# A masked row sum with a loop of as many rounds as the lengths need: addresses worked out on one partition, rests behind the first blocks, TensorE's program on a 256 boundary

## The chip, the cores and the metric

One core of one Trainium2 chip. The metric is the device time of the kernel in microseconds (us), the median of several runs; each timed run stands beside runs of the kernel before on the same chip.

## The reference

```python
B, S, D = 8, 8192, 512
x: (B, S, D) float32, lengths: (B,) in 16..S-1, w: (D, D) float32
masked = x * (pos < lengths)
cs = cumsum(masked, axis=1)
out = cs[b, lengths[b] // 2, :] @ w          # (8, 512)
```

So row b of the result is the sum of the first n[b] = min(lengths[b]//2 + 1, lengths[b]) rows of x[b], times w. For this draw n is 570, 2690, 256, 2057, 905, 3772, 3859, 571. The kernel reads only these rows: whole blocks of 512 rows (1 MB), and rests of under 512 rows.

## The kernel before

TensorE sums a block with matmuls whose stationary operand is a column of weights (which of the 8 rows the block belongs to). The first block of rows 0 and 1 is loaded blind, before the lengths are known. One block of row 7 is loaded into a tile `last` at the end. All other blocks are "places": 7 buffers, used in rounds of 7. With these lengths there are 25 places (the two blind ones and 23 more), so four rounds hold them; the longest lengths need nine.

```python
BLIND, NS = 2, 7
ROUNDS = -(-(B * S // 2 // BLK - 1) // NS)          # 9
...
# SyncE: loads
sp.wait_ge(s_dve, DVE_ADDR)
sp.load(facts, meta[:])                              # how many places, ...
with sp.Fori(0, ROUNDS):
    sp.load(at, addr[:, off:off + NS])               # seven addresses to registers
    nested(sp, left, NS, load_item)                  # load_item waits for s_free[k], starts a DMA
    ...
    sp.wait_ge(s_dve, DVE_ALL)
... then the two halves of `last`
# VectorE, before the loops: n_f (lengths to counts, one partition); TensorE broadcasts them to
# 128 partitions (n_ps); then on 128 partitions
step(dve.tensor_copy, out=cnt[:], in_=n_ps[:, :B])
step(dve.tensor_scalar, out=blocks[:], in0=cnt[:], ...)
... has, usual, begin, step_a, since, part_a, sum_a, addr[0:7], meta x3      # = DVE_ADDR
... bit masks for the rests, since for all places, wtab (weights of all places)   # = DVE_MASK
# GpSimd: waits for n_f, then memset of the second rest buffer (128 x 2048)
# TensorE
pe.wait_ge(s_dve, DVE_MASK)
with pe.Fori(0, ROUNDS):
    with pe.If_cmp(rest_rounds, 1, "IS_GE"): ...     # the rests of two rows, 8 matmuls
    nested(pe, left, NS, add_item)   # add_item: 2 idle matmuls, wait s_full[k], 4 matmuls
    ...
tell()                               # a tiny matmul that signals VectorE: the sum is complete
... first half of last; fold of the copied sum; second half of last; product with w
```

`keep_busy` in front of each place is a pair of idle matmuls, meant to keep TensorE's clock up (in the nine rounds below, one more pair in each round took the tail from 4.20 us to 3.33). A float32 matmul appears in the trace as two passes: 8 records for the 4 of a place, 16 for the 8 of two rests.

## Time and profile before

| | before |
|---|---|
| time, median of the runs | 93.1 us (93.07 to 94.05) |
| span of the profiled run | 90.7 us |
| DMA | 345 GB/s mean over the span, 419 to 420 while it streams |
| TensorE busy | 53.3 us (59%) |
| last two DMAs of `last` landed | 78.73 and 79.96 us |
| output issued | 87.8 us |

How to read it: the share of busy time says little here. What counts is whether DMA streams without gaps to its end, and how long the chain is from the last landing to the output. The lines are in the prediction below.

### The profile page before, as it was taken

The page shows a single profiled execution, that of the slowest core. Times are in us where ns is not written, and L with a number is a line of the kernel's source. Part 1 is how long each engine was busy: PE and PEld are TensorE (multiplying, and loading weights), DVE is VectorE, ACT ScalarE, POOL GpSimd, SP SyncE. Part 2 cuts the span into 40 slices and gives each one's busy share as a digit, 9 for nine tenths or more (in the row PEclk, how much of TensorE's full clock was granted, in tenths as well). Part 3 has the DMA queues.
Part 4 walks back from the last instruction along what each step waited for, and adds up shares of the span by engine and source line. Part 5 has one row for each costly group of instructions (what it writes and reads, how often), then busy time and mean ns, then how long its engine had stood idle before and what let it go on. Part 6 is the DMA issues. An engine that isn't in the chain of part 4 may idle for free. (4 is left out here: it accounts for less than half of the span.)

```text
span 90.7 us, 1568 instructions
## 1 busy us (share of the span) xinstructions
PE 53.3 (59%) x387; PEld 11.6 (13%) x391; DVE 17.5 (19%) x86; ACT 3.7 (4%) x5; POOL 3.0 (3%) x11
## 2 busy tenths in 40 slices
PE   0730006999999994242668993354659966404840
PEld 0400001111112110000012110010112111003520
DVE  3787886010101110000000110000000000003220
ACT  3900000000000000000000000000000000000020
POOL 5700000000000000000000000000000000000000
PEclk9999999999999999999999999999999999997597
DMA  2899989999999999999999999999999999400000
GB/s 29 340 416 426 369 288 413 437 419 416 434 408 423 416 423 430 415 395 426 412 423 430 416 416 430 408 426 416 419 423 426 419 419 407 177 2 0 0 0 7
DMA packets 4837, 31.28 MB, mean 345 GB/s; under 512 B 674, under 2 KB 690, under 8 KB 1218
## 3 DMA queue, kind: packets, MB, share of 16 engines
q1 hardware_dynamic: 3906, 27.27, 73.0%
q10 hardware_dynamic: 928, 3.97, 11.3%
q8 instruction: 1, 0.02, 0.1%
q14 instruction: 2, 0.02, 0.0%
HBM read 31.23 MB, written 0.02 MB: 345 GB/s over the span
## 5 line engine op out<-in xcount | busy, mean ns | idle before, releaser
L430 PE MATMUL s_ps<-xt,cur 128*8 128x512 f32 x200 | 26.1, 593 | 16.5 <-PEq L131 16.4
L430 PE MATMUL s_ps<-rem,cur_rem 128*8 128x512 f32 x64 | 9.3, 707 | 9.1 <-PEq L131 9.1
L443 PE MATMUL idle_ps<-idle 128*128 128x512 bf16 x46 | 14.2, 384 | 0.6 <-issue 0.6
L404 DVE COPY cur<-wtab 128x8 f32 x18 | 3.1, 171 | 36.3 <-DVEq L131 36.3
L430 PEld LDWEIGHTS s_ps<-xt,cur 128*8 128x8 f32 x200 | 3.4, 87 | 27.8 <-issue 27.8
L443 PEld LDWEIGHTS idle_ps<-idle 128*128 128x128 bf16 x50 | 2.8, 97 | 22.3 <-issue 22.3
L289 DVE COPY s_sb<-s_ps 128x256 f32<-128x256 f32 x2 | 0.8, 425 | 21.7 <-PE idle_ps L447 21.7
L262 ACT COPY o_sb<-o_ps 8x128 f32<-8x128 f32 x2 | 0.5, 260 | 82.5 <-PE o_ps L504 82.5
L430 PEld LDWEIGHTS s_ps<-rem,cur_rem 128*8 128x8 f32 x64 | 1.8, 95 | 15.8 <-issue 15.7
L447 PE MATMUL idle_ps<-idle 128*1 128x1 bf16 x1 | 0.2, 163 | 4.2 <-issue 4.2
L451 PE MATMUL n_ps<-n_f,ones 1*128 1x8 f32 x2 | 0.6, 366 | 2.9 <-DVE n_f L289 2.9
L436 PE MATMUL t_ps<-last,e_last 128*8 128x128 f32 x32 | 2.3, 414 | 0.0
L397 DVE COPY cur_rem<-table 128x32 f32 x6 | 1.1, 182 | 5.8 <-DVEq L131 5.8
L452 PE MATMUL s_ps<-zero 1*128 1x512 f32 x2 | 2.0, 1126 | 0.0
L214 ACT ACTIVATE rem<-rem 128x2048 uint32<-128x2048 uint32 x1 | 1.9, 1910 | 0.0
L278 POOL MEMSET rem<- 128x2048 f32 x1 | 1.8, 1805 | 0.8 <-DVE n_f L289 0.8
L504 PE MATMUL o_ps<-wt,t_sb 128*8 128x128 f32 x32 | 1.2, 304 | 0.4 <-DVE t_sb L289 0.4
L214 ACT ACT_TABLE_LOAD x1 | 1.3, 1283 | 1.3 <-PEq L525 1.3
L436 PEld LDWEIGHTS t_ps<-last,e_last 128*8 128x8 f32 x32 | 1.3, 121 | 0.2
L289 DVE TENSOR_TENSOR wtab<-since 128x504 f32<-128x504 f32 x1 | 1.1, 1066 | 0.0
L289 DVE TENSOR_TENSOR part_a<-since,step_a 1x49 f32<-1x49 f32 (+1 forms) x2 | 1.1, 529 | 0.1
L504 PEld LDWEIGHTS o_ps<-wt,t_sb 128*8 128x8 f32 x32 | 0.9, 98 | 1.0 <-issue 0.9
(62 smaller groups left out, 14.3 us busy)
## 6 DMA issues: line engine op xcount, KB each, us to landing
xt<-in_x_dram SPq DMA_DIRECT2D x25, 1024.0 KB, 16.6
rem<-in_x_dram ACTq DMA_DIRECT2D x3, 512.0 KB, 7.5
wt<-in_w_dram ACTq DMA_DIRECT2D x1, 1024.0 KB, 4.9
last<-in_x_dram SPq DMA_DIRECT2D x2, 512.0 KB, 6.9
rem<-in_x_dram ACTq DMA_DIRECT2D x3, 256.0 KB, 7.0
rem<-in_x_dram ACTq DMA_DIRECT2D x3, 128.0 KB, 6.7
rem<-in_x_dram ACTq DMA_DIRECT2D x3, 32.0 KB, 5.5
rem<-in_x_dram ACTq DMA_DIRECT2D x1, 64.0 KB, 7.2
```

Source lines behind the costliest of these rows:

```text
L214: act.memzero(rem[:, 0]).then_inc(s_rfree[0], 1)
L262: copy = act.copy(out=o_sb[1][:, j * P:(j + 1) * P], in_=o_ps[64 + 32 * j:64 + 32 * j + B, :P])
L278: pool.memset(rem[:, 1], 0.0).then_inc(s_rfree[1], 1)
L289: do(*args, **kw).then_inc(s_dve, 1)
L397: dve.tensor_copy(out=cur_rem[:, q], in_=rests[:, ds(dve.snap(at, min_val=1, max_val=B // 2 - 1), 1), q].rearrange("p o w -> p (o w)"),).t ...
L404: dve.tensor_copy(out=cur[:, k], in_=wtab[:, ds(dve.snap(at, min_val=1, max_val=ROUNDS - 1), 1), k].rearrange("p o b -> p (o b)"),).then_i ...
L430: return pe.matmul(s_ps[32 * j:32 * j + B], lhsT=weights, rhs=rows, start=False, stop=False, skip_group_check=True, tile_position=(0, 32 * j))
L436: return pe.matmul(t_ps[32 * j:32 * j + B, :P], lhsT=weights, rhs=row[:, P * j:P * (j + 1)], start=False, stop=False, skip_group_check=Tru ...
L443: pe.matmul(idle_ps[:], lhsT=idle[:, :P], rhs=idle[:], start=True, stop=True)
L451: pe.matmul(n_ps[:, :B], lhsT=ones[:], rhs=n_f[:], start=True, stop=True).then_inc(s_pe, 1)
L452: pe.matmul(s_ps[:], lhsT=zero[:], rhs=zero[:, :1].to_broadcast((1, D)), start=True, stop=False, skip_group_check=True)
L504: mm = pe.matmul(o_ps[32 * j:32 * j + B, :P], lhsT=t_sb[:, kc, :B], rhs=wt[:, kc, j * P:(j + 1) * P], start=(kc == 0), stop=(kc == KC - 1) ...
```

## The change

Its intent: no empty rounds; first addresses sooner; the two blind blocks used first, so that their buffers come free early; and TensorE's program put on a 256 boundary, with the product in a block of its own and a branch hint. Cut to its core:

```diff
-        sp.wait_ge(s_dve, DVE_ADDR)
-        sp.load(facts, meta[:])
-        with sp.Fori(0, ROUNDS):
+        sp.wait_ge(s_dve, DVE_ADDR)
+        sp.load([left] + at[BLIND:], addr[:, BLIND - 1:NS])
+        nested(sp, left, NS, load, BLIND)
+        sp.wait_ge(s_dve, DVE_ALL)
+        sp.load(facts, meta[:])
+        with sp.Fori(1, facts[1]):                      # rounds needed, at least 4
 # GpSimd
-        pool.wait_ge(s_dve, DVE_N)
+        pool.wait_ge(s_dve, DVE_ADDR)
         pool.memset(rem[:, 1], 0.0)
 # VectorE
+        begins(n_i, blocks1, has1, usual1, begin1)      # on one partition, straight from n_i
+        ... step_a, since, part_a, sum_a, addr for five places    # = DVE_ADDR, step 21 (was 28)
+        step(dve.tensor_copy, out=n_f[:], in_=n_i[:])   # = DVE_N, step 23 (was 11)
+        ... bit masks; cnt; begins() on 128 partitions; weights of round 0 (no table wtab any more)
+        ... number of rounds = max(4, rounds with a place in them) into meta
 # TensorE
+        pe.addr_align(256, offset=0, max_nops=0)
+        hint = pe.mark_branch_hint_location()
-        with pe.Fori(0, ROUNDS):
+        with pe.Fori(0, rounds):
+            nested(pe, left, BLIND, add_item)
             ... rests of two rows
-            nested(pe, left, NS, add_item)
+            nested(pe, left, NS, add_item, BLIND)
-        ... product
+        pe.br("product")
+        with nc.body("product", ...): ... product; pe.br("product_end").branch_hint(hint)
```

VectorE's refills follow the same order (weights of two places, rests, weights of five).

More of the change, by code (lines that the diff above doesn't have):

```diff
@@ L6 @@
 from concourse._compat import with_exitstack
+from concourse.ordered_engine_set import OrderedEngineSet
 F32 = mybir.dt.float32
@@ L80 @@
     idle = sb("idle", [P, D], BF16)
-    cnt = sb("cnt", [P, B], I32)
-    blocks = sb("blocks", [P, B], I32)
     special = sb("special", [P, B])
-    has = sb("has", [P, B])
-    usual = sb("usual", [P, B])
     one8 = sb("one8", [P, B])
-    begin = sb("begin", [P, B + 1])
+    cnt, blocks, has, usual, begin = [sb(n, [P, B + (n == "begin")], I32 if n in ("cnt", "blocks") else F32)
+                                      for n in ("cnt", "blocks", "has", "usual", "begin")]
+    blocks1, has1, usual1, begin1 = [sb(n + "1", [1, B + (n == "begin")], I32 if n == "blocks" else F32)
+                                     for n in ("blocks", "has", "usual", "begin")]
     step_c = sb("step_c", [1, B - 1])
@@ L96 @@
     addr = sb("addr", [1, ITEMS], I32)
-    meta = sb("meta", [1, 3], I32)
-    wtab = sb("wtab", [P, ROUNDS, NS, B])
+    left_f = sb("left_f", [1, ROUNDS])
+    round_f = sb("round_f", [1, 1])
+    meta = sb("meta", [1, 4], I32)
     cur = sb("cur", [P, NS, B])
@@ L142, in less @@
         eng.reg_alu(n, n, 0, ALU.max)
-    DVE_SEL, DVE_N, DVE_ADDR, DVE_MASK, DVE_ALL = 2, 11, 28, 51, 56
+    DVE_SEL, DVE_ADDR, DVE_N, DVE_MASK, DVE_ALL = 2, 21, 23, 56, 64
     DVE_LAST = DVE_ALL + 6
@@ L168, in _, with load @@
         at = [sp.alloc_register(f"sp_at{k}") for k in range(NS)]
-        facts = [sp.alloc_register(f"sp_fact{k}") for k in range(3)]
-        sp.reg_mov(off, 0)
+        facts = [sp.alloc_register(f"sp_fact{k}") for k in range(4)]
+        sp.reg_mov(off, NS)
+        def load(k):
+            take(sp, s_free[k], 1)
+            sp.dma_start(
+                out=xt[:, k], in_=xf[ds(sp.snap(at[k]), BLK)].rearrange("(p g) d -> p g d", g=G)
+            ).then_inc(s_full[k], 16)
         sp.wait_ge(s_dve, DVE_ADDR)
+        sp.load([left] + at[BLIND:], addr[:, BLIND - 1:NS])
+        nested(sp, left, NS, load, BLIND)
+        sp.wait_ge(s_dve, DVE_ALL)
         sp.load(facts, meta[:])
-        sp.reg_mov(left, facts[0])
-        with sp.Fori(0, ROUNDS):
-            sp.load(at, addr[:, ds(sp.snap(off, min_val=0, max_val=ITEMS - NS), NS)])
-            def load(k):
-                take(sp, s_free[k], 1)
-                sp.dma_start(
-                    out=xt[:, k], in_=xf[ds(sp.snap(at[k]), BLK)].rearrange("(p g) d -> p g d", g=G)
-                ).then_inc(s_full[k], 16)
-            def load_item(k):
-                if k < BLIND:
-                    with sp.If_cmp(off, 1, "IS_GE"):
-                        load(k)
-                else:
-                    load(k)
-            nested(sp, left, NS, load_item)
+        with sp.Fori(1, sp.snap(facts[1], min_val=B // 2, max_val=ROUNDS)):
+            sp.load(at, addr[:, ds(sp.snap(off, min_val=NS, max_val=ITEMS - NS), NS)])
             less(sp, left, NS)
+            nested(sp, left, NS, load)
             sp.reg_alu(off, off, NS, ALU.add)
             sp.reg_alu(off, off, ITEMS - NS, ALU.min)
-            sp.wait_ge(s_dve, DVE_ALL)
-        with sp.If_cmp(facts[1], 1, "IS_GE"):
-            from_rows = xf[ds(sp.snap(facts[2]), BLK)].rearrange("(p g) d -> p g d", g=G)
+        with sp.If_cmp(facts[2], 1, "IS_GE"):
+            from_rows = xf[ds(sp.snap(facts[3]), BLK)].rearrange("(p g) d -> p g d", g=G)
             for h in range(2):
@@ L307, in _, with begins, sinces @@
         step(dve.tensor_scalar, out=n_i[:], in0=n_i[:], scalar1=1, scalar2=None, op0=ALU.add)
-        step(dve.tensor_tensor, out=n_f[:], in0=n_i[:], in1=lens1[:, ::2], op=ALU.min)
-        assert done == DVE_N, done
-        step(dve.memset, since[:, :1], 1.0)
-        step(dve.memset, since[:, B:], 0.0)
-        step(dve.memset, e_last[:], 0.0)
-        step(dve.memset, e_last[:, B - 1:], 1.0)
-        dve.wait_ge(s_pe, 1)
-        step(dve.tensor_copy, out=cnt[:], in_=n_ps[:, :B])
-        step(dve.tensor_scalar, out=blocks[:], in0=cnt[:], scalar1=9, scalar2=None,
-             op0=ALU.logical_shift_right)
-        step(dve.scalar_tensor_tensor, out=has[:], in0=blocks[:], scalar=1.0, in1=special[:],
-             op0=ALU.is_ge, op1=ALU.mult)
-        step(dve.tensor_tensor, out=usual[:], in0=blocks[:], in1=has[:], op=ALU.subtract)
-        step(dve.tensor_tensor_scan, out=begin[:, 1:], data0=one8[:], data1=usual[:], initial=float(BLIND),
-             op0=ALU.mult, op1=ALU.add)
-        step(dve.scalar_tensor_tensor, out=step_a[:], in0=usual[:1, :B - 1], scalar=float(-BLK), in1=step_c[:],
-             op0=ALU.mult, op1=ALU.add)
+        step(dve.tensor_tensor, out=n_i[:], in0=n_i[:], in1=lens1[:, ::2], op=ALU.min)
+        def begins(cnt, blocks, has, usual, begin):
+            parts = blocks.shape[0]
+            step(dve.tensor_scalar, out=blocks[:], in0=cnt[:], scalar1=9, scalar2=None,
+                 op0=ALU.logical_shift_right)
+            step(dve.scalar_tensor_tensor, out=has[:], in0=blocks[:], scalar=1.0, in1=special[:parts],
+                 op0=ALU.is_ge, op1=ALU.mult)
+            step(dve.tensor_tensor, out=usual[:], in0=blocks[:], in1=has[:], op=ALU.subtract)
+            step(dve.tensor_tensor_scan, out=begin[:, 1:], data0=one8[:parts], data1=usual[:],
+                 initial=float(BLIND), op0=ALU.mult, op1=ALU.add)
+        def sinces(begin, a, b):
+            parts = begin.shape[0]
+            step(dve.tensor_tensor, out=since[:parts, 1:B, a:b],
+                 in0=shape(item[:parts, a:b].unsqueeze(1), parts, B - 1, b - a),
+                 in1=shape(begin[:, 1:B].unsqueeze(2), parts, B - 1, b - a), op=ALU.is_ge)
         def addresses(a, b):
@@ L332, in addresses @@
             step(dve.tensor_tensor, out=addr[:, a:b], in0=item_a[:, a:b], in1=sum_a[:, a:b], op=ALU.add)
-        def sinces(parts, a, b):
-            step(dve.tensor_tensor, out=since[:parts, 1:B, a:b],
-                 in0=shape(item[:parts, a:b].unsqueeze(1), parts, B - 1, b - a),
-                 in1=shape(begin[:parts, 1:B].unsqueeze(2), parts, B - 1, b - a), op=ALU.is_ge)
+        begins(n_i, blocks1, has1, usual1, begin1)
+        step(dve.tensor_copy, out=addr[:, BLIND - 1:BLIND], in_=begin1[:, B:])
+        step(dve.scalar_tensor_tensor, out=step_a[:], in0=usual1[:, :B - 1], scalar=float(-BLK), in1=step_c[:],
+             op0=ALU.mult, op1=ALU.add)
         dve.wait_ge(s_pool, 1)
-        sinces(1, 0, NS)
-        addresses(0, NS)
-        step(dve.tensor_copy, out=meta[:, :1], in_=begin[:1, B:])
-        step(dve.tensor_copy, out=meta[:, 1:2], in_=has[:1, B - 1:])
-        step(dve.tensor_scalar, out=meta[:, 2:], in0=blocks[:1, B - 1:], scalar1=BLK,
-             scalar2=(B - 1) * S - BLK, op0=ALU.mult, op1=ALU.add)
+        sinces(begin1, BLIND, NS)
+        addresses(BLIND, NS)
         assert done == DVE_ADDR, done
+        step(dve.memset, since[:, :1], 1.0)
+        step(dve.tensor_copy, out=n_f[:], in_=n_i[:])
+        assert done == DVE_N, done
         step(dve.memset, bits[:], 256)
@@ L362, in _ @@
         step(dve.tensor_tensor, out=thr[:, 2:], in0=thr_i[:], in1=shape(m4[:], P, 2), op=ALU.mult)
+        step(dve.memset, since[:, B:], 0.0)
+        dve.wait_ge(s_pe, 1)
+        step(dve.tensor_copy, out=cnt[:], in_=n_ps[:, :B])
+        begins(cnt, blocks, has, usual, begin)
+        sinces(begin, 0, ITEMS)
+        step(dve.tensor_tensor, out=cur[:].rearrange("p k b -> p b k"), in0=since[:, :B, :NS],
+             in1=since[:, 1:, :NS], op=ALU.subtract)
+        step(dve.memset, cur[:, :BLIND], 0.0)
+        step(dve.tensor_copy, out=cur[:, :BLIND].rearrange("p k b -> p (k b)")[:, ::B + 1], in_=has[:, :BLIND])
         step(dve.memset, table[:], 0.0)
@@ L370, in _ @@
         step(dve.tensor_copy, out=cur_rem[:], in_=rests[:, 0])
-        sinces(P, 0, ITEMS)
-        step(dve.tensor_tensor, out=wtab[:].rearrange("p r k b -> p b (r k)"), in0=since[:, :B],
-             in1=since[:, 1:], op=ALU.subtract)
-        step(dve.memset, wtab[:, 0, 1, :1], 0.0)
-        for b in range(BLIND):
-            step(dve.tensor_copy, out=wtab[:, 0, b, b:b + 1], in_=has[:, b:b + 1])
-        step(dve.tensor_copy, out=cur[:], in_=wtab[:, 0])
-        step(dve.memset, t_ps[:, :P], 0.0)
+        step(dve.tensor_copy, out=meta[:, :1], in_=begin1[:, B:])
+        step(dve.tensor_scalar, out=left_f[:], in0=item[:1, :ROUNDS], scalar1=float(-NS), scalar2=begin1[:, B:],
+             op0=ALU.mult, op1=ALU.add)
+        step(dve.tensor_scalar, out=left_f[:], in0=left_f[:], scalar1=1.0, scalar2=None, op0=ALU.is_ge)
+        step(dve.tensor_reduce, out=round_f[:], in_=left_f[:], axis=mybir.AxisListType.X, op=ALU.add)
+        step(dve.tensor_scalar, out=meta[:, 1:2], in0=round_f[:], scalar1=float(B // 2), scalar2=None, op0=ALU.max)
+        step(dve.tensor_copy, out=meta[:, 2:3], in_=has1[:, B - 1:])
+        step(dve.tensor_scalar, out=meta[:, 3:], in0=blocks1[:, B - 1:], scalar1=BLK,
+             scalar2=(B - 1) * S - BLK, op0=ALU.mult, op1=ALU.add)
         assert done == DVE_MASK, done
         addresses(NS, ITEMS)
+        step(dve.memset, t_ps[:, :P], 0.0)
+        step(dve.memset, e_last[:], 0.0)
+        step(dve.memset, e_last[:, B - 1:], 1.0)
         step(dve.tensor_scalar, out=fold_i[:], in0=fold_i[:], scalar1=31, scalar2=None,
@@ L386, in _, with weights @@
         dve.wait_ge(s_dve, done)
-        left, at, rest_rounds = [dve.alloc_register(f"dve_{n}") for n in ("left", "at", "rests")]
-        dve.load([left], meta[:, :1])
-        dve.reg_mov(at, 1)
+        left, rounds, at, of, rest_rounds = [dve.alloc_register(f"dve_{n}") for n in ("left", "rounds", "at", "of", "rests")]
+        dve.load([left, rounds], meta[:, :2])
+        dve.reg_mov(at, NS)
+        dve.reg_mov(of, 1)
         dve.reg_mov(rest_rounds, B // 2 - 1)
-        with dve.Fori(1, ROUNDS):
+        with dve.Fori(1, dve.snap(rounds, min_val=B // 2, max_val=ROUNDS)):
             less(dve, left, NS)
+            def weights(k):
+                take(dve, s_done[k], 1)
+                here = ds(dve.snap(at, min_val=NS, max_val=ITEMS - NS) + k, 1)
+                dve.tensor_tensor(
+                    out=cur[:, k], in0=since[:, :B, here].rearrange("p b o -> p (b o)"),
+                    in1=since[:, 1:, here].rearrange("p b o -> p (b o)"), op=ALU.subtract,
+                ).then_inc(s_free[k], 1)
+            nested(dve, left, BLIND, weights)
             with dve.If_cmp(rest_rounds, 1, "IS_GE"):
@@ L398, in _ @@
                         out=cur_rem[:, q],
-                        in_=rests[:, ds(dve.snap(at, min_val=1, max_val=B // 2 - 1), 1), q].rearrange("p o w -> p (o w)"),
+                        in_=rests[:, ds(dve.snap(of, min_val=1, max_val=B // 2 - 1), 1), q].rearrange("p o w -> p (o w)"),
                     ).then_inc(s_rfree[q], 1)
-            def weights(k):
-                take(dve, s_done[k], 1)
-                dve.tensor_copy(
-                    out=cur[:, k],
-                    in_=wtab[:, ds(dve.snap(at, min_val=1, max_val=ROUNDS - 1), 1), k].rearrange("p o b -> p (o b)"),
-                ).then_inc(s_free[k], 1)
-            nested(dve, left, NS, weights)
+            nested(dve, left, NS, weights, BLIND)
             less(dve, rest_rounds, 1)
-            dve.reg_alu(at, at, 1, ALU.add)
-            dve.reg_alu(at, at, ROUNDS - 1, ALU.min)
+            dve.reg_alu(at, at, NS, ALU.add)
+            dve.reg_alu(at, at, ITEMS - NS, ALU.min)
+            dve.reg_alu(of, of, 1, ALU.add)
+            dve.reg_alu(of, of, B // 2 - 1, ALU.min)
         dve.wait_ge(s_pe, PE_ALL)
@@ L448, in tell, with add_item @@
                       stop=True).then_inc(s_pe, 1)
+        pe.addr_align(256, offset=0, max_nops=0)
+        hint = pe.mark_branch_hint_location()
+        pe.wait_ge(s_dve, DVE_SEL)
+        pe.matmul(s_ps[:], lhsT=zero[:], rhs=zero[:, :1].to_broadcast((1, D)), start=True,
+                  stop=False, skip_group_check=True)
         pe.wait_ge(s_dve, DVE_N)
         pe.matmul(n_ps[:, :B], lhsT=ones[:], rhs=n_f[:], start=True, stop=True).then_inc(s_pe, 1)
-        pe.matmul(s_ps[:], lhsT=zero[:], rhs=zero[:, :1].to_broadcast((1, D)), start=True,
-                  stop=False, skip_group_check=True)
         pe.wait_ge(s_pool, 2)
         pe.wait_ge(s_dve, DVE_MASK)
-        left, has_last = pe.alloc_register("pe_left"), pe.alloc_register("pe_has")
+        left, rounds, has_last = [pe.alloc_register(f"pe_{n}") for n in ("left", "rounds", "has")]
         rest_rounds = pe.alloc_register("pe_rests")
-        pe.load([left, has_last], meta[:, :2])
+        pe.load([left, rounds, has_last], meta[:, :3])
         pe.reg_mov(rest_rounds, B // 2)
-        with pe.Fori(0, ROUNDS):
+        with pe.Fori(0, pe.snap(rounds, min_val=B // 2, max_val=ROUNDS)):
+            def add_item(k):
+                keep_busy()
+                take(pe, s_full[k], 16)
+                for j in range(G):
+                    mm = add(j, cur[:, k], xt[:, k, j])
+                mm.then_inc(s_done[k], 1)
+            nested(pe, left, BLIND, add_item)
             with pe.If_cmp(rest_rounds, 1, "IS_GE"):
@@ L466, in _ @@
                     mm.then_inc(s_rdone[q], 1)
-            def add_item(k):
-                keep_busy()
-                take(pe, s_full[k], 16)
-                for j in range(G):
-                    mm = add(j, cur[:, k], xt[:, k, j])
-                mm.then_inc(s_done[k], 1)
-            nested(pe, left, NS, add_item)
+            nested(pe, left, NS, add_item, BLIND)
             less(pe, left, NS)
@@ L498, in _ @@
             tell()
-        pe.wait_ge(s_w, 16)
-        for kc in range(KC):
-            if kc % 2 == 0:
-                pe.wait_ge(s_dve, DVE_ALL + 3 + kc // 2)
-            for j in range(4):
-                mm = pe.matmul(o_ps[32 * j:32 * j + B, :P], lhsT=t_sb[:, kc, :B],
-                               rhs=wt[:, kc, j * P:(j + 1) * P],
-                               start=(kc == 0), stop=(kc == KC - 1), tile_position=(0, 32 * j))
-        mm.then_inc(s_pe, 1)
+        pe.br("product")
+        with nc.body("product", valid_engines=OrderedEngineSet([mybir.EngineType.PE])):
+            pe.wait_ge(s_w, 16)
+            for kc in range(KC):
+                if kc % 2 == 0:
+                    pe.wait_ge(s_dve, DVE_ALL + 3 + kc // 2)
+                for j in range(4):
+                    mm = pe.matmul(o_ps[32 * j:32 * j + B, :P], lhsT=t_sb[:, kc, :B],
+                                   rhs=wt[:, kc, j * P:(j + 1) * P],
+                                   start=(kc == 0), stop=(kc == KC - 1), tile_position=(0, 32 * j))
+            mm.then_inc(s_pe, 1)
+            pe.br("product_end").branch_hint(hint)
+        nc.switch_bb("product_end")
     block.__exit__(None, None, None)
```

## The prediction

> **What bounds the kernel now.** I read the busy slices first, then stretches of time, the chain of waits, the timeline of the first 13 us, and the branches of TensorE. The kernel streams rows of x from HBM in places of 512 rows (1 MB), seven to a round, and adds them up on TensorE.
>
> Slices and stretches (span, PE, PEld, DVE, ACT, POOL busy; clock; DMA share; GB/s):
>
> ```profile
> DMA  2899989999999999999999999999999999400000
> 9.07:11.30 2.23, 0.00 (x0) 0.00 (x0) 1.94 (x7) 0.00 (x0) 0.00 (x0) 1.00 1.02 375
> 11.30:13.60 2.30, 0.00 (x0) 0.00 (x0) 2.00 (x7) 0.00 (x0) 0.00 (x0) 1.00 0.80 284
> 18.10:66.00 47.90, 33.76 (x229) 5.67 (x232) 3.99 (x23) 0.00 (x0) 0.00 (x0) 1.00 1.01 419
> 78.20:82.80 4.60, 0.45 (x7) 0.00 (x0) 0.00 (x0) 0.00 (x0) 0.00 (x0) 1.00 0.03 11
> 82.80:87.80 5.00, 3.83 (x73) 2.68 (x73) 1.91 (x6) 0.52 (x2) 0.00 (x0) 0.66 0.00 0
> ```
>
> From 2.3 to 78.2 us the DMA engines are full at 419 GB/s, except for one dip at 9 to 13.6 us. Then 4.6 us pass in which neither DMA nor TensorE has much to do, and the last 5 us run at a mean clock of 0.66. So there are three places where time can be had: the dip, the hole and the slow tail.
>
> The chain of waits (start, length, what):
>
> ```profile
> 77.61 1.05 PE s_ps L430 x8
> 78.65 4.18 issue
> 82.83 0.16 PE idle_ps L447
> 82.99 2.45 PE t_ps L436 x40
> ...
> 85.87 1.29 PE o_ps L504 x32
> ```
>
> The hole is 4.18 us of "issue" on TensorE: no wait, only its sequencer. The loop runs nine rounds. The lengths of this draw give 25 places plus one block that goes to `last`, so four rounds hold them all and five are empty. The branches of the loop show the five (operation, count, duration in ns min/median/max, first and last start):
>
> ```profile
> L461 PEldq COMPARE_BRANCH  x9: 64/201/201, 14.2 to 82.0; - x9
> L460 PEldq COMPARE_BRANCH  x9: 69/201/223, 27.8 to 82.7; - x9
> ```
>
> In an empty round three branches are taken at 201 ns each, with the register operations and gaps some 0.92 us per round in the trace (back edges at 78.05, 79.01, 79.93, 80.84, 81.75 and 82.71). Five make 4.65 us, of which 0.5 lies under the last matmuls.
>
> The dip: timeline of the address chain, the competing memset and SyncE's loads:
>
> ```profile
> 2.90 1.80 POOL L278 MEMSET rem<- 128x2048 f32 x1 [0.82 <-DVE n_f L289]
> 3.59 0.17 DVE L289 CAST cnt<-n_ps 128x8 int32<-128x8 f32 x1
> 3.79 0.94 DVE L289 TENSOR_SCALAR blocks<-cnt 128x8 int32<-128x8 int32 x1
> 4.77 0.17 DVE L289 SCALAR_TENSOR_TENSOR has<-blocks,special 128x8 f32<-128x8 int32 x1
> ...
> 10.04 3.09 SPq L179 DMA_DIRECT2D xt<-in_x_dram  x5
> ...
> L175 SPq TENSOR_LOAD <-addr x9: 934/1467/1488, 8.2 to 70.5; - x9
> ...
> 72.13 0.87 SPq L200 DMA_DIRECT2D last<-in_x_dram  x2
> DMA to landing us min/median/max: 6.6/6.9/7.3
> ```
>
> The first computed place is issued at 10.04, its data flow from about 12.0, but the two blind blocks are through at 10.3. And `last` is issued only at 72.13, 10.2 us after the last place (61.61), because SyncE too walks five empty rounds with a register load in each. It lands at 78.73 and 79.96, still before TensorE wants it at 82.98.
>
> [...]`blocks` took 944 ns where others of 128x8 take 168, and ended at 4.74, when the memset (2.90 + 1.80) ended. [...]the clock records have 0.5 from 82.88 to 86.29, right after the hole. [...] The TensorE trace before shows no such stall (empty rounds are 0.92 us each, all alike), so its alignment and branch hint have nothing visible to remove[...].
>
> **The change part by part.**
>
> *Addresses from one partition.* The chain no longer passes through TensorE (broadcast, then copy `cnt`) and no longer runs beside the memset, which now waits for the addresses. From the end of `n_f` at 2.85: ten steps on one partition at about 0.19 us (their durations are 0.14 to 0.23 plus 0.035 gap) make DVE_ADDR near 4.9 instead of 7.04. SyncE then loads one set of six registers (0.9) instead of two sets (877 and 946 ns), and skips the two pairs of branches for blind places. First issue: 4.95 + 0.9 + 0.3 = 6.2 instead of 10.04; its data flow from about 8.1, before 10.3. So the dip closes: lost bytes are (419-375) x 2.23 + (419-284) x 2.30 = 409 KB, at 419 GB/s **0.98 us** earlier for everything the stream delivers.
>
> *What this gives back.* The 1.8 us memset now starts near 5.0 and should block the cast of `n_f` until about 6.8. VectorE then has 33 further steps to DVE_MASK. With their measured durations (twelve bit steps 2.14, since 0.65, cur 0.25 instead of wtab's 1.07, table to cur_rem 1.0, seven small meta steps 1.3 and the rest) I get 13.7, against 13.08 before. TensorE starts near 15.2 instead of 14.48. That is off the path: it starts with the blind blocks, so place 0 is free near 17.6, and SyncE, after DVE_ALL near 16.1 and two register loads, reissues at about 18.6, against 20.31 before. The queue then has bytes until about 23.
>
> *Rests behind the blind blocks.* Moves 3.6 us of cold matmuls from ahead of the first place; frees two places earlier and delays the next rest loads by some 3 us. They have slack: rests of round 1 landed by 26.94 and would be used after 30. Worth 0 by itself.
>
> *Rounds as needed.* Four rounds instead of nine. The tell follows the last matmul at once: -4.02 us of the hole. VectorE and SyncE lose their empty rounds too; `last` is issued near 62, but queued behind the same bytes, so it lands with the end of the stream: 79.96 - 0.98 = 79.0.
>
> *Tail, worked out.* Last place lands at 77.47 - 0.98 = 76.5; its matmuls end at 77.65; tell 77.8; s_sb copies (2 x 0.425) end at 78.7; first half of `last` in between; fold to 78.95; second half at 79.0. With no hole the clock stays full, so those 16 matmuls start within 0.45 us instead of 0.8 and end at 79.65, against 85.43 before: 5.78 us earlier. The product has 8 of its 32 matmuls at half clock now: about 0.15 less, perhaps 0.3 with its first weight load. The rest (copies, output, end) is as before, 5.25 - 0.2. Span: 79.65 + 5.05 = 84.7. The timed figure is 93.1 for a span of 90.7; adding the same 2.4 gives **87.1**, I put 87.0.
>
> In parts: dip 1.0, hole net of the new wait for `last` and of overlap about 3.8, full clock in the tail about 1.2: 6.0.
>
> **The rivals.** (a) *A fetch stall takes the place of the empty rounds.* With them gone the exit runs straight from a loop of some 215 instructions into new code. For it: [...]that the author adds alignment and a hint. Against it: the back edges at 28.3, 48.9 and 68.3 show no stall[...].[...] (b) *The stream's end doesn't move*, because the memset, the later TensorE start or later rests open another dip at 20 to 25 us. The margin (reissue 18.6, bytes until 23) speaks against it; then 88. (c) *The end of `last` is later*, since it now sits 10 us longer in the queue among rests: at most some tenths, 87.5. (d) *The nine rounds were hidden under the stream anyway*: the hole is after the stream's end at 78.2, and only 1.8 us of it lie before `last` lands at 79.96; then the 2.9 us from 79.96 to 82.83 are still gained, and the time could not be above 90.3.
>
> **Range and chances.** Centre 87.0. Everything as worked out, or a bit better in the end sequence, gives 86; rival (b)[...] 88 to 89.2. Range 85.9 to 89.3. Faster by over 2% needs under 91.2[...]: 0.97; within 2%: 0.02; slower: 0.01.
>
> **What would show it.** Right: DMA share full in the slices of 9 to 13.6 us; first place issued near 6.2; no long idle ahead of the tell; clock 1.0 until the product; `last` issued near 62 and TensorE's second half of it waiting for the landing near 79.0. `n_f` stretched to about 1.7 us beside the memset. Wrong: an "issue" piece of over 1 us in the chain between the last place and the product[...], a dip at 20 to 25 us, or a clock of 0.5 in the tail again.

## The result, and the profile after

86.72 us (86.61 to 86.74), against 93.1 before: ratio 0.9289, 95% interval 0.923 to 0.9348. A ratio compares the fast runs of both kernels in the same rounds, so it is not quite the ratio of the medians. On a second chip the same kernel gave 87.17 against 93.18, ratio 0.9343 (0.9293 to 0.9393): faster by some 6.5 to 7%.

Slices and stretches of the kernel after (span, then PE, PEld, DVE, ACT, POOL busy; clock; DMA share; GB/s):

```profile
PEclk9999999999999999999995799999997556999999
DMA  2899999999999999999999999999999999993000
9.07:11.30 2.23, 0.00 (x0) 0.00 (x0) 1.85 (x9) 0.00 (x0) 0.00 (x0) 1.00 1.03 412
11.30:13.60 2.30, 0.00 (x0) 0.00 (x0) 1.87 (x11) 0.00 (x0) 0.00 (x0) 1.00 1.00 419
```

The dip is closed (412 and 419 GB/s where 375 and 284 stood). The clock is full in the tail (1.00 from 77.96 to 81.40), and in this run falls to half lie in mid-stream instead.

The chain of waits of the kernel after:

```profile
76.90 0.98 PE s_ps L449 x8
77.88 0.08 PE idle_ps L466
77.96 0.02 issue
77.98 0.44 DVE s_sb L290
...
78.92 0.96 PE t_ps L455 x20
...
80.30 1.10 PE o_ps L529 x32
```

The 4.18 us of issue are gone: the tell follows the last place at once, and from the tell's end (77.96) to the end of the t_ps stage (79.88) it takes 1.92 us at full clock where 2.45 stood. No piece of issue over 0.14 us is left between the last place and the product, so nothing stalls the exit.

Timeline of the kernel after: the memset, the cast behind it, and SyncE's issues:

```profile
4.97 1.80 POOL L279 MEMSET rem<- 128x2048 f32 x1 [2.88 <-DVE addr L290]
4.99 0.11 DVE L290 MEMSET since<- 128x63 f32 x1
5.13 1.66 DVE L290 CAST n_f<-n_i 1x8 f32<-1x8 int32 x1
...
6.79 53.06 SPq L181 DMA_DIRECT2D xt<-in_x_dram  x23
60.91 0.87 SPq L201 DMA_DIRECT2D last<-in_x_dram  x2
```

First place at 6.79 instead of 10.04; `last` at 60.91 instead of 72.13. One line of the list of DMA issues does not fit the rest (before, the same transfer had 4.9 us):

```profile
wt<-in_w_dram ACTq DMA_DIRECT2D x1, 1024.0 KB, 7.4
```

This transfer is issued at the very start in both kernels, and nothing in the change touches it. The experiments found out why it is 2.5 us later.

### The profile page after: what moved, and what is told of

It is laid out like the page before. It is cut to its first block, busy times and chain, and to the rows that moved or that the text cites.

```text
span 84.9 us, 1511 instructions
## 1 busy us (share of the span) xinstructions
PE 56.6 (67%) x387; PEld 10.8 (13%) x391; DVE 18.7 (22%) x94; ACT 3.7 (4%) x5; POOL 3.0 (4%) x11
## 5 line engine op out<-in xcount | busy, mean ns | idle before, releaser
L449 PE MATMUL s_ps<-xt,cur 128*8 128x512 f32 x200 | 30.2, 679 | 10.4 <-PEq L138 10.4
L462 PE MATMUL idle_ps<-idle 128*128 128x512 bf16 x46 | 16.4, 436 | 8.9 <-DVE addr L290 8.3
L413 DVE TENSOR_TENSOR cur<-since 128x8 f32 x18 | 3.1, 173 | 34.7 <-DVEq L138 34.7
L449 PE MATMUL s_ps<-rem,cur_rem 128*8 128x512 f32 x64 | 7.6, 592 | 0.0
L290 DVE CAST n_f<-n_i 1x8 f32<-1x8 int32 x1 | 1.7, 1656 | 0.0
L455 PE MATMUL t_ps<-last,e_last 128*8 128x128 f32 x32 | 1.2, 273 | 0.1
L476 PEld LDWEIGHTS n_ps<-n_f,ones 1*128 1x128 f32 x2 | 0.5, 308 | 4.8 <-DVE n_f L290 4.8
L290 DVE TENSOR_TENSOR part_a<-since,step_a 1x35 f32<-1x35 f32 (+1 forms) x2 | 1.0, 518 | 0.1
L290 DVE TENSOR_TENSOR since<-item,begin 1x35 f32<-1x35 int32 (+1 forms) x2 | 0.8, 401 | 0.1
```

What stands on the lines that cost most here:

```text
L290: do(*args, **kw).then_inc(s_dve, 1)
L413: dve.tensor_tensor(out=cur[:, k], in0=since[:, :B, here].rearrange("p b o -> p (b o)"), in1=since[:, 1:, here].rearrange("p b o -> p (b o ...
L449: return pe.matmul(s_ps[32 * j:32 * j + B], lhsT=weights, rhs=rows, start=False, stop=False, skip_group_check=True, tile_position=(0, 32 * j))
L455: return pe.matmul(t_ps[32 * j:32 * j + B, :P], lhsT=weights, rhs=row[:, P * j:P * (j + 1)], start=False, stop=False, skip_group_check=Tru ...
L462: pe.matmul(idle_ps[:], lhsT=idle[:, :P], rhs=idle[:], start=True, stop=True)
L476: pe.matmul(n_ps[:, :B], lhsT=ones[:], rhs=n_f[:], start=True, stop=True).then_inc(s_pe, 1)
```

## The experiments

Twelve runs (eleven edited kernels, and the kernel after once more), each timed in five rounds. All give a correct result.

### Four rounds in the kernel before

```diff
-        with sp.Fori(0, ROUNDS):      (and the same for VectorE and TensorE)
+        with sp.Fori(0, B // 2):
```

> The kernel before with its three loops run four times instead of nine, nothing else. My theory (empty rounds and the clock they let fall are most of the gain; the earlier first addresses are worth only the dip): the last data land near 79.96 as before, the tell follows the last matmul near 78.8, the clock stays full, span about 85.7 and time about 87.5. Rival (the early addresses carry the gain, the hole was hidden by the wait for the last block): 90 or more.

Measured: 87.77 us, ratio 0.9424 (0.9386 to 0.9462), span 85.6, last landing 79.86. Its chain:

```profile
77.50 1.04 PE s_ps L430 x8
78.55 0.07 PE idle_ps L447
...
79.58 0.99 PE t_ps L436 x20
```

As expected: this edit alone gives some 5.5 us of the 6 to 6.4. The hole was not hidden by the wait for the last block.

### Nine rounds in the kernel after, and nine rounds with a warm clock

```diff
-  out=meta[:, 1:2], in0=round_f[:], scalar1=float(B // 2), op0=ALU.max
+  out=meta[:, 1:2], in0=round_f[:], scalar1=float(ROUNDS), op0=ALU.max
   # second kernel, besides: keep_busy() at the end of every TensorE round
```

> The changed kernel with the number of rounds forced to nine. My theory: five empty rounds of 0.92 us come back behind the last place, 4.0 us of hole, the clock falls to half in the tail; the tell near 81.9, span about 89.8, time about 91.7 (0.8 to 1.0 under the kernel before: the dip alone). Rival (order of rests and addresses matter more): under 90.

> As the one with nine rounds, and a pair of idle matmuls at the end of every round, so that the clock does not fall in the empty ones. If the half clock of the tail costs what I said (1.2 us in the 24 t_ps and the first product matmuls), this is 0.7 to 1.2 us faster than the nine rounds alone, near 90.7; if the clock is not on the path, the same as those.

Measured: 94.06 us (ratio 1.0088) for the nine rounds, and 93.43 us (0.9999, 0.9957 to 1.0041) for the three fast runs of the warm kernel; its other three were slow (the median of all six: 94.08). The first is 2.4 us above what I expected. Its chain:

```profile
77.88 5.69 issue
83.58 0.16 PE idle_ps L466
83.74 2.46 PE t_ps L455 x40
...
86.62 1.32 PE o_ps L529 x32
```

The hole is 5.69 us, not 4.0. In the trace an empty round is now about 1.23 us (back edges at 77.29 and 83.44, five rounds), with four taken branches of 208 ns and more instead of three of 201, since the places stand in two groups with the rests between. Rests behind the blind blocks thus make an empty round dearer; without empty rounds no cost of it shows (87.17 us against 87.24 with the rests first, below).

The warm kernel keeps the clock at 1.0 through the hole:

```profile
78.73 0.97 PE idle_ps L462 x4
...
84.68 0.11 PE idle_ps L466
84.81 0.44 DVE s_sb L290
...
85.75 0.85 PE t_ps L455 x20
...
87.02 1.10 PE o_ps L530 x32
```

From the tell's end (83.74 and 84.79) to the product's end (87.94 and 88.12) it takes 3.33 us instead of 4.20: half clock in the tail costs **0.87 us**. As a whole the warm kernel's fast runs are 0.6 us faster than the nine rounds by the medians and 0.8 by the ratios, about the lower end of the 0.7 to 1.2 that I expected; the absolute 90.7 missed with the longer rounds. In the profiled pair the product ends no earlier (88.12 against 87.94), for two reasons. The idle matmuls do not lie beside the branches but behind them (0.6 busy and 0.72 issue a round in the chain), so the hole is 5.95 us (78.73 to 84.68) instead of 5.69. And the last place's matmuls end 0.85 us later (78.73 against 77.88), after half clock from 65.48 to 72.31. So 0.87 rests on the chain of one profiled run of each.

### Alignment and hint, together and apart

```diff
 # a_noalign: all three out; a_nohint: only alignment kept; a_hintonly: only alignment out
-        pe.addr_align(256, offset=0, max_nops=0)
-        hint = pe.mark_branch_hint_location()
-        pe.br("product") ... with nc.body("product") ... branch_hint(hint)
```

> The changed kernel without the 256 alignment, the branch hint and the separate product block. My theory (no fetch stall was visible before): the same as the changed kernel within 0.3 us, 86.7. Rival (the exit of the loop now meets code that is not there): [...]with a piece of issue in the chain between the last place and the product.

Measured: **85.9 us**, ratio 0.9209 (0.9186 to 0.9232): neither the same nor slower, but some 0.8 us faster. No stall at the exit: the last place's matmuls end at 77.17 and the tell at 77.24:

```profile
76.13 1.04 PE s_ps L449 x8
77.17 0.07 PE idle_ps L466
77.24 0.02 issue
```

What differs is at the start. Each of these transfers raises its semaphore 16 times; the profile counts 16 DMA engines, and one of the 16 is called a queue below. The increments of the transfer of `w`, read from the trace (us):

```
after       5.12 5.18 5.22 ... 5.67 5.71   8.26
a_noalign   5.40 5.41 5.43 ... 5.66 5.68   5.70
```

One of the 16 comes 2.55 us after the others. In the DMA records of the kernel after a packet of 16,384 bytes of kind "instruction" runs from 2.96 to 3.90; without alignment and hint there is none of that size before 77 us.

The lateness of this transfer overstates how far the queue is behind. A packet of 8 KB takes 0.31 us at the median here. After 5.6 us only four packets of `w` are left, and they start at 5.62, 5.93, 6.54 and 7.16: from the second on one comes in every other slot of 0.31 us, while the packets of x flow. So I estimate from these four packets of 0.31 us that the late queue is some 1.2 us behind; that the increment is later still goes with the slots in between, 0.61 to 0.62 us from one start to the next. At the end of the stream the lag is 0.99 us in this kernel (78.18 and 79.17 in the table further down). The packet of 0.94 us is about as long, but the two do not simply match: in a_nohint below, the packet takes 1.47 us and the lag at the end is 0.47.

I then took the two apart:

> The changed kernel with the 256 alignment kept, without the hint and the separate product block. What is disputed: in the changed kernel one of the 16 increments of the first weights transfer lands at 8.26 us and the other 15 by 5.71, and a 16 KB instruction packet runs at 2.96 to 3.90; without alignment and hint both are gone and the time is 0.8 us less. If the hint makes that packet: no packet near 3 us, all 16 by about 5.8, 85.9 us. If the alignment's jump makes it: the late increment stays, 86.7 us.

> The counterpart: hint and product block kept, no alignment. If the hint makes the early packet: late increment near 8, 86.7 us. If the alignment does: all 16 by about 5.8, 85.9 us.[...]

Measured: alignment alone 86.68 us (0.9302), late increment at 7.99, packet at 2.16 to 3.63. Hint alone 86.16 us (0.9246), all 16 by 5.73, no early packet. So the alignment makes the packet and the late increment; the hint does neither, and no use of it shows here. All eight profiles of kernels with the alignment show both, and none of the four without it. The difference in time on this chip, 0.5 us, is small beside the intervals (0.9264 to 0.9339 and 0.92 to 0.9291, which overlap); the other comparisons show 0.8 us (above) and 1.35 (the last experiment).

### GpSimd's memset one step later

```diff
-        pool.wait_ge(s_dve, DVE_ADDR)
+        pool.wait_ge(s_dve, DVE_N)
```

> The changed kernel with GpSimd's memset of the second rest buffer waiting for the cast of n_f too. If that cast is stretched to 1.66 us by the memset, it takes 0.15 now, and as the operations behind it are memsets and one-element tensor_scalars, nothing else is stretched: mask ready 1.5 us earlier, TensorE starts near 14.1. As I held that this is off the path, the time stays within 0.3 us of the changed kernel, 86.7. Rival: TensorE's start matters, 85.3.

Measured: 86.79 us (0.9309), beside 86.68 of the other aligned kernel on this chip. Its timeline:

```profile
5.14 0.16 DVE L290 CAST n_f<-n_i 1x8 f32<-1x8 int32 x1
...
5.35 1.80 POOL L279 MEMSET rem<- 128x2048 f32 x1 [3.27 <-DVE n_f L290]
...
5.59 0.15 DVE L290 TENSOR_SCALAR m<-pid 128x1 int32<-128x1 int32 x1
...
14.18 1.02 PE L462 MATMUL idle_ps<-idle 128*128 128x512 bf16 x2 [8.24 <-DVE addr L290]
```

The cast takes 0.16 instead of 1.66 us, the operations beside the memset are not stretched (`m`, with one element a partition, took 0.15 us at 5.59 beside it, and 0.15 without it at 7.08 in the kernel after), TensorE starts 1.5 us earlier (14.18 against 15.70), and the time does not move. What the change gives back on VectorE is off the path.

### The dip put back, with and without the alignment

```diff
-        sp.wait_ge(s_dve, DVE_ADDR)
+        sp.wait_ge(s_dve, DVE_ADDR + 10)      # a_sp_held; a_noalign_held: besides, no alignment
```

> The changed kernel with SyncE held until ten steps of VectorE after the addresses, so that the first computed place is issued near 10.0 us as before. My theory (the dip is worth 0.8 to 1.0): the dip at 10 to 13 us returns, last data land near 80.0, 87.6 us. Rival (the dip was hidden): 86.7.

Measured: 86.88 us (0.9324). The first place is issued at 10.07, the dip is back, and yet it costs only 0.1 to 0.2 us by the medians beside 86.68 and 86.79 of the other aligned kernels on this chip, and 0.4 in the profiled runs (86.92 against 86.56 and 86.52). The intervals of the ratios are some 0.35 us to either side, so it may be anything from nothing to half a microsecond. My expected 87.6 was wrong. The stretches of this kernel:

```profile
9.07:11.30 2.23, 0.00 (x0) 0.00 (x0) 1.85 (x9) 0.00 (x0) 0.00 (x0) 1.00 1.01 374
11.30:13.60 2.30, 0.00 (x0) 0.00 (x0) 1.87 (x11) 0.00 (x0) 0.00 (x0) 1.00 0.94 288
```

> The changed kernel without alignment and hint, and with SyncE held so that the dip returns. In the aligned kernel the held addresses cost only 0.2 us (79.35 against 79.17 at the last landing) although the stream as a whole was 1.0 us behind. Theory S (every transfer needs all 16 DMA queues; the alignment's early 16 KB packet holds one of them back by 2.5 us, that one is never idle in the dip, and it alone sets the landing): without the alignment no queue is late, so the dip costs its full 0.8 to 1.0 us, time about 86.8, last landing about 79.4. Theory T (the dip is simply hidden, the two costs add): 85.9 + 0.2 = 86.1.

Measured: 86.99 us (0.9319), beside 85.9 (other chip) and 86.16 (alignment out, hint kept, other chip), and 85.82 for an unaligned kernel with a split `last` on this chip: the dip costs 0.8 to 1.2 us without the alignment. That is theory S and not T. The increments of the last transfer (second half of `last`) show it increment by increment, with the instruction packet of 16 KB that lies in the stream:

| kernel | 16 KB packet | 15th increment | 16th | time |
|---|---|---|---|---|
| before (dip) | at 51.65 | 79.44 | 79.96 | 93.1 |
| b_rounds4 (dip; chip 3) | at 51.21 | 79.08 | 79.86 | 87.77 |
| after | at 2.96 | 78.18 | 79.17 | 86.72 |
| a_nohint (aligned; chip 2) | at 2.16 | 78.42 | 78.89 | 86.68 |
| a_sp_held (dip, aligned; chip 2) | at 2.16 | 79.26 | 79.35 | 86.88 |
| a_noalign (chip 3) | none before 77 | 78.20 | 78.48 | 85.9 |
| a_noalign_split (`last` in four; chip 10) | none before 77 | 78.19 | 78.28 | 85.82 |
| a_noalign_held (dip; chip 10) | none before 78 | 79.29 | 79.35 | 86.99 |

Compare kernels on one chip. With the alignment the dip moves the 15th increment by 0.84 us (a_sp_held against a_nohint) and the last one by 0.46. Without it (a_noalign_held against a_noalign_split) it moves them by 1.10 and 1.07. (Against after and a_noalign, on other chips, the last one moves by 0.18 and 0.87.) TensorE waits for all 16: in the kernel after it began on the second half of `last` at 79.22, behind the 16th at 79.17. My reading of these numbers: the early packet holds back one of the 16 queues from 3 us on; that queue still has bytes to move during the dip while the others run dry, so dip and packet hide each other in large part, and it is mostly the later of the two that shows at the end. How late the last increment is differs among the aligned kernels without the dip, from 0.47 us (a_nohint) to 1.38 (a_rests_first), so the exact share hidden is not settled. That the late increment of every transfer belongs to the same queue is inferred (the records do not number the queues); that packet and late increment come and go with the alignment is shown.

### Rests first again

```diff
 # TensorE and VectorE: rests ahead of both groups of places in each round
```

> The changed kernel with the rests ahead of the blind blocks in each round, as before, on TensorE and in VectorE's refills. I held that the order is worth nothing by itself because queued bytes cover it: same as the changed kernel within 0.3 us. Rival: the first two places come free 3 us later, the stream runs dry near 23 us, up to 1 us longer. In both TensorE's empty branches are one fewer per round.

Measured: 87.24 us (0.9345, 0.9294 to 0.9396), beside 87.17 of the kernel after on the same chip: no effect of the order shows within the intervals, some 0.5 us to either side.

### A candidate, and the kernel after once more

```diff
 # a_noalign, and:
-            for h in range(2):  sp.dma_start(out=last[:, 2*h:2*h+2], ...).then_inc(s_last[h], 16)
+            for g in range(G):  sp.dma_start(out=last[:, g:g+1], ...).then_inc(s_last[g], 16)
```

> Candidate for a faster version: without alignment and hint, and the last block loaded in four parts of 256 KB instead of two of 512 KB, each with its own semaphore. What follows its landing is then 8 matmul passes instead of 16: 0.2 us less than without alignment alone, 85.7. Rival: runs of 2 KB instead of 4 KB per partition slow the end of the stream: 85.9 or more.

> The changed kernel itself on the chip of these runs, as the base for differences of some tenths: ratio near 0.929, last landing near 79.2, one late increment in the first transfers.

Measured: 85.82 us, ratio 0.9205 (0.9158 to 0.9251), and 87.17 us, 0.9343. The candidate is 1.35 us under the kernel after on the same chip. The split itself shows nothing beyond leaving the alignment out (0.9205 against 0.9209 for a_noalign): in its chain TensorE's t_ps stage starts at 77.88, right after VectorE's copies of the sum, which are the longer way by now. The simpler a_noalign is the version I would keep, for these lengths.

## Why the prediction was right

The time, 87.0 predicted and 86.72 measured, and the main mechanism are right; two steps are not: what the dip is worth, and that the alignment costs nothing.

- **Empty rounds.** Right. The hole is gone; four rounds alone give 5.5 us. As a bound, "no more than 90.3" held easily.
- **Clock in the tail.** Right in kind, its term too large: 1.2 us predicted, 0.87 measured between cold and warm. In the change itself the same stretch, from the tell's end to the product's end, went from 4.17 us (82.99 to 87.16) to 3.44 (77.96 to 81.40).
- **First addresses.** First issue 6.79 instead of 6.2: the load of six registers took 1.46 us, not the 0.9 I took from the lower end of a row of 934 to 1488. It was early enough, and the dip closed.
- **"0.98 us earlier for everything the stream delivers"** failed as a step. The stream as a whole did gain that: the bytes that it has moved by 76 us are ahead of those of the kernel before by what 420 GB/s carry in 0.96 us. But the last landing came 0.79 earlier, and the run that put the dip back shows that only part of it is due to the dip: with the alignment in, the dip is worth 0.1 to 0.2 us by the medians and 0.4 to 0.5 at the last landing. I summed bytes over 16 queues where the last of the 16 increments decides (79.17 in the kernel after, 0.99 us behind the 15th). That the number came out near the predicted one is partly luck: the kernel before has a 16 KB packet too, at 51.65, behind the dip, so both its costs add up. The increments of b_rounds4, which has that packet at 51.21, bear this out: the 16th comes 0.06 us after the 15th in the place that lands at 50.01, and 0.95 us after it in the one that lands at 59.80. No run took that packet out by itself.
- **Alignment and hint.** I wrote that they have nothing visible to remove. Right: without them there is no stall either (a_noalign: no piece of issue over 0.14 us from the last place to the product), so rival (a), a stall that no trace here shows, does not happen in any version with four rounds. But I gave them no cost. The alignment costs 0.5 to 0.8 us: 86.68 against 86.16 on one chip, 86.72 against 85.9 on two. On a third chip the kernel after and the split kernel without alignment lie 1.35 us apart, so it may be more.
- **VectorE's later mask, rests' order.** Right: `n_f` stretched to 1.66 (1.7 predicted), off the path (86.79 without the stretch), order worth 0 within the noise (87.24 against 87.17). The delay of the rests was too small in the prediction: the loads for the second round began at 22.76 instead of 17.51 and had landed by 31.91 instead of 26.93, 5 us later and not 3. TensorE began on them at 33.17, so the slack was still enough.
- **Clock of 0.5 in mid-stream.** Not foreseen. In the profiled run after it is at half from 44.3 to 47.8 and from 64.8 to 71.6, and TensorE then works back to back until 77.9. It costs little: of the four runs of the kernel, the one with mean clock 0.994 took 86.61 and those with 0.94 to 0.96 took 86.70 to 86.74. The hint is not the reason: single runs of a_nohint have mean clocks of 0.94 and of 0.994, as runs of the kernel after do. The records show what goes with a fall. Its four changes in mid-stream (44.34, 47.75, 64.82, 71.65) lie whole multiples of 3.41 us apart, and in the stretch of that length before each of the two falls (40.93 to 44.34 and 61.41 to 64.82) TensorE was busy for 0.72 and 1.40 us; in the stretches between them it was busy for 2.20 us or more. In the profiled run of a_nohint, at full clock, it never fell under 1.58 us from 35.92 to 66.63. Whether the waits for a place gather in one such stretch or are shared by two may thus decide; no run tests it.
- **Three readings were loose.** The 2.4 us added to the span set the median time (93.1) against the span of a run that itself took 92.72; in one run the two differ by 2.0 before and 1.8 after, so the sum should have given 86.7. The span itself was 84.9, with 84.7 predicted. DMA was not full from 2.3 us on: 2.27 to 4.50 ran at 338 GB/s, share 0.81. And beside the memset (2.90 to 4.70) only `blocks` was stretched (0.94 us): the cast of `cnt`, shown above at 3.59, took 0.17 us while it ran.

## What to carry to other kernels

Look for the stretch in which neither DMA nor the bound engine works. Here it was the 4.6 us behind the stream's end: the empty rounds, with three taken branches of 201 ns in each, stood in it with 4.18 us, and four rounds alone took 5.5 us off the time. A transfer that was spread over 16 queues ended here with the last of 16 increments, up to 1.38 us behind the 15th: read that one, not the mean GB/s, and when a gap closes without effect, ask which queue was not waiting in it. A placement of instructions can bring a transfer with it (here a packet of 16 KB at 2.96, in kernels that took 0.5 to 0.8 us longer), so try it out and in before keeping it.

## Register loads and branches as measured

- The time of a register load did not follow the number of registers: seven took 934 to 1494 ns, six 1462, four 313, three 957 and 877, two 718 and 776, one 557.
- In the empty rounds of the kernel before, TensorE's compare-and-branch took 201 to 207 ns where it was taken, and 69 ns where it fell through at their end; in those of the nine rounds in the kernel after, two of the lines show medians of 208 and 214 ns, with 67 and 78 as the shortest.
